# Dummy matmuls before and between the first transposes of a two-layer mixer trunk: 13 become 16 + 2 + 4

## The chip, the cores and the metric

One core of a Trainium2 chip. The metric is the device time of one launch in microseconds, the median of several launches.

## The reference

A decoder trunk of two layers on 256 tokens of width 1024, batch 1. Each layer normalizes the stream, projects it once, feeds four token mixers from the projection (sparse attention, a gated short convolution, stick-breaking attention and an S5 state-space layer), gates and merges them, projects the sum and adds it back:

```python
h = rms_norm(x, g)
proj = h @ w_in          # split by columns among the mixers, the silu gates and the merge gates
y = [nsa(...), conv(...), stickbreak(...), s5(...)]     # each [1, 256, 256]
m = sum(sigmoid(gate_i) * ((y_i * silu(z_i)) @ w_branch_i) for i in range(4))
x = x + m @ w_out
```

The S5 mixer multiplies its input into a complex state (`bu`), runs a diagonal recurrence over the 256 positions, multiplies the states back and sums them (`s5acc`), and passes the result through a GLU.

## The kernel before

All matrix products are taken in a split form: each float32 operand is cut into a high part (`hi`, a cast) and a low part (`lo`, operand minus `hi`), and three products hi·hi, hi·lo, lo·hi are summed. The weights stream in slots of 512 KB (536 KB for the first two) through the DMA queue of SyncE (SP): `raw`, three buffers; the cast to `hi` (L148, ScalarE or VectorE) and the subtraction `lo` (L150, VectorE, some on GpSimd), five buffers each. Slots 0 and 1 hold the query weights `q`, 2 and 3 `ksw`, and so on. Slot 0 holds the rows of the weights that meet the first 512 columns of h, slot 1 the other 512.

The beginning of layer 0: x is loaded, `norm_square` and `norm_scale` make the normalized h for the first 128 rows (t = 0) in two halves of 512 columns (L553, VectorE); `norm_transpose` turns each half by four transposing matmuls (`hT`, L561), copies the result out as `hh` (L564, ScalarE) and subtracts to get `hl` (L565, VectorE). Then the products of q and ksw (L488) begin, and the second 128 rows (t = 1) follow. While TensorE has nothing to do at the start, 13 matmuls of a zero tile (`warm_ps`, 128x128 by 128x512, bf16) run on it. Their output is not used.

In the middle of a layer the S5 mixer forms a chain over eight blocks, in the order 00, 01, 04, 05, 02, 03, 06, 07: TensorE makes `bu` (L855), VectorE multiplies it by tables (`s5a`, `s5b`, L858 and L859), GpSimd adds (L286, L289), VectorE scans (L865) and multiplies (`cy`, L868 and L871), GpSimd adds again, and after four blocks TensorE sums them into `s5acc` (L883). GpSimd starts the adding of a block's `s5a` behind the `cy` of the block before. After both groups of four come `s5yT`, `s5y`, the GLU (`glu`, L905) and `s5th` (L914). `spawn(prepare(l + 1))` behind it loads the next layer's parameters (`pk`) and computes its tables on GpSimd, ScalarE and VectorE, in among layer 0's merging (`mg`: merge gates; `br`: branch projections; `g`: the gates' tanh, L928; `mt`, L946).

The orders of the DMA queue (SP) and of GpSimd are those in which the program was written. The orders of TensorE, VectorE and ScalarE are chosen by a scheduler that plays the program through on a cost model of its own and always takes the ready instruction it judges best; every instruction added to one of these engines can move others.

Of the kernel before, what the change touches and what calls it, by code (L numbers as in the profile page):

```python
# [9 lines left out]
F32 = mybir.dt.float32  # L10
# [7 lines left out]
P = 128  # L18
# [17 lines left out]

_PK = [("a_re", 8), ("a_im", 8), ("ldt", 8), ("pe", 32), ("b_re", 128), ("b_im", 128), ("c_re", 128), ("c_im", 128),
       ("d", 2), ("glub", 4), ("convw", 6), ("w2", 64), ("qkg", 256), ("qkgs", 256)]
WARM = 13
PK, _o = {}, 0  # L40
for _n, _w in _PK:
    PK[_n] = (_o, _w)
# [135 lines left out]
def tile_hybrid_trunk(ctx: ExitStack, tc: tile.TileContext, x, pos, cst, msk, wq, ws, ng, pk, w1, gw, out):  # L178
    nc = tc.nc
    V, A, G, T = nc.vector, nc.scalar, nc.gpsimd, nc.tensor  # L180
# [11 lines left out]
    pj = ctx.enter_context(tc.tile_pool(name="pj", bufs=4, space=PSUM))  # L192
# [24 lines left out]
    def small(name, cols):  # L217
        t = sp.tile([P, 16], F32, tag="s", name=name)
        return t[:, :cols]
# [39 lines left out]
    ident = C("ident")  # L259
# [295 lines left out]
    def norm_transpose(l, t, act):  # L555
        hh, hl = act
        h = Ls[l]["norm"][t][0]
        for c in range(2):
            ps = wk.tile([P, 4, P], F32, tag="w", name=f"hT{l}{t}{c}")
            for k in range(4):  # L560
                T.transpose(ps[:, k, :], h[:, (4 * c + k) * P:(4 * c + k + 1) * P], ident)  # L561
            dst = (slice(None), slice(4 * c, 4 * c + 4), slice(t * P, (t + 1) * P))
            with tc.high_priority():
                A.copy(hh[dst], ps)  # L564
                V.tensor_sub(hl[dst], ps, hh[dst].bitcast(F32))  # L565
# [449 lines left out]

    warm = cp.tile([P, P], BF16, name="warm")
    V.memset(warm, 0.0)
    ps = pj.tile([P, 512], F32, tag="pj", name="warm_ps")
    for _ in range(WARM):
        T.matmul(ps, lhsT=warm, rhs=warm[:, None, :].to_broadcast([P, 4, P]), start=True, stop=True)  # L1020
    sin0 = small("sin0", 1)
    A.activation(sin0, halfpi, AF.Sin)
    act = new_act(0)
# [3 lines left out]
    for c in range(2):  # L1027
        norm_square(0, 0, c, 2)
    norm_scale(0, 0)
    norm_transpose(0, 0, act)  # L1030
    W.advance(-3)
    rope = rope_tables()
# [16 lines left out]
    for l in range(DEPTH):  # L1049
# [36 lines left out]
        qs = get_n(l, "q")  # L1086
        n_part(l, "q", qs, act, 0, q_done, WQ, by_pass=True)
        norm_transpose(l, 1, act)
        ks = get_n(l, "ksw")
        pump()  # L1090
# [61 lines left out]
        if more:  # L1152
            W.advance((l + 1) * NSLOT - 1)
        out_part(l, 3, s3, mx, 1, lambda: norm_transpose(l + 1, 0, act) if more else None)
        done_n(l, ("wo", 3))
        if more:
# [85 lines left out]
def build(arrays):  # L1242
    import concourse.bacc as bacc

    nc = bacc.Bacc("TRN2", target_bir_lowering=False, num_devices=1)
    args = [nc.dram_tensor(f"in_{k}_dram", a.shape, mybir.dt.from_np(a.dtype), kind="ExternalInput").ap()
            for k, a in arrays.items()]
    args.append(nc.dram_tensor("out_0_dram", (S, D), F32, kind="ExternalOutput").ap())
    with tile.TileContext(nc, schedule_with_timeline_sim=True) as tc:
        tile_hybrid_trunk(tc, *args)  # L1250
    return nc
# [9 lines left out]
```

## Time and profile before

| | us |
|---|---|
| median of 3 runs | 568.13 (567.42 to 570.21) |
| the profiled execution | 566.94 |
| its span | 565.2 |
| TensorE busy in it | 546.1 |
| TensorE's mean granted clock in it | 0.987 of full speed |

The span is the time between the first and the last instruction of the profiled execution; 1.74 us lie around it. Times in the rows below are microseconds from the start of the span. A granted clock of 1.00 is TensorE's level of 2.4 GHz, 0.50 that of 1.2 GHz. A bracket such as `[2.56 <-DVE h L553]` says that the engine sat idle for 2.56 us before the row and that VectorE's h ended it.

### The profile page before, as it was taken

What the parts mean: (1) busy time and instruction counts of PE and PEld (TensorE: products, weight loads), DVE (VectorE), ACT (ScalarE), POOL (GpSimd) and SP (SyncE); (2) the same over time, 40 slices, a digit from 0 to 9 for tenths busy, and PEclk for the clock granted to TensorE, in tenths of its full rate; (3) what the DMA queues carried; (4) which work ended last, traced back from release to release, by engine and by line L of the source; (5) the groups of instructions that cost most, each with busy time, mean ns of one, the idle gap of its engine ahead of it and who ended that gap; (6) DMA issues with size and microseconds to landing.
All of it is one profiled execution on the core that took longest, in us unless ns stands there. A gap on an engine that the chain in (4) does not pass through costs nothing.

```text
span 565.2 us, 11178 instructions
## 1 busy us (share of the span) xinstructions
PE 546.1 (97%) x4417; PEld 510.1 (90%) x4417; DVE 440.1 (78%) x654; ACT 264.0 (47%) x436; POOL 275.3 (49%) x309
## 2 busy tenths in 40 slices
PE   6999999999899899799999999999999999999997
PEld 3898988889799799799998998889889999999997
DVE  3999776888989764888769985968898777687772
ACT  4656353654334444654454555454434345444440
POOL 7949536634665529597033776713335620243200
PEclk7899999999899999999999999999999999999999
DMA  7584154544444636465556725364344635555541
GB/s 257 194 279 157 42 201 119 199 153 146 150 126 137 223 134 206 149 199 180 190 171 213 220 72 164 112 222 135 112 154 147 202 139 180 187 188 186 188 135 53
DMA packets 28853, 93.54 MB, mean 166 GB/s; under 512 B 3968, under 2 KB 5248, under 8 KB 28800
## 3 DMA queue, kind: packets, MB, share of 16 engines
q1 hardware_dynamic: 28800, 92.82, 50.5%
q8 instruction: 35, 0.57, 0.4%
q14 instruction: 18, 0.15, 0.1%
HBM read 88.61 MB, written 1.05 MB: 159 GB/s over the span
## 4 chain that ended last, share of the span: by engine, by line
PE 71%; DVE 11%; POOL 9%; issue 4%; DMA 2%; ACT 2%; SPq 1%; DVEq 0%; POOLq 0%; ACTq 0%
PE mg L498 24%; PE wo L488 7%; PE br L943 7%; PE z L498 4%; DVE lo L150 2%; PE s5u L498 2%; PE sbv L488 2%; PE bg L498 2%; PE sc L709 2%; PE xin L498 2%; PE sbk L498 2%; PE nsacc L746 2%; DVE s5b L865 1%; POOL cy L286 1%; PE cg L498 1%
## 5 line engine op out<-in xcount | busy, mean ns | idle before, releaser
L150 DVE TENSOR_TENSOR lo<-raw,hi 128x1024 fp32r<-128x1024 f32 (+1 forms) x152 | 209.1, 1379 | 43.8 <-ACT hi L148 43.4
L148 ACT CAST hi<-raw 128x1024 fp32r<-128x1024 f32 (+1 forms) x154 | 161.2, 1050 | 173.8 <-PE mg L498 52.8
L498 PE MATMUL mg<-hh,hi 128*128 128x256 f32 x512 | 145.1, 283 | 0.4 <-DVE mt L946 0.4
L498 PE MATMUL mg<-hh,lo 128*128 128x256 f32 x512 | 144.6, 283 | 0.0
L498 PE MATMUL mg<-hl,hi 128*128 128x256 f32 x512 | 144.5, 282 | 0.0
L498 PEld LDWEIGHTS mg<-hh,hi 128*128 128x128 f32 x512 | 97.0, 190 | 3.0 <-issue 2.4
L498 PEld LDWEIGHTS mg<-hl,hi 128*128 128x128 f32 x512 | 97.4, 190 | 1.2 <-issue 1.2
L498 PEld LDWEIGHTS mg<-hh,lo 128*128 128x128 f32 x512 | 97.0, 189 | 1.2 <-issue 1.2
L286 POOL TENSOR_TENSOR mt<-mt,mt 128x512 f32<-128x512 f32 x12 | 19.0, 1585 | 70.6 <-DVE mt L946 70.6
L289 POOL TENSOR_TENSOR cy<-cy 128x256 f32<-128x256 f32 x16 | 18.2, 1138 | 57.9 <-DVE cy L871 54.2
L488 PE MATMUL wo<-hi,mx 128*128 128x256 f32 x256 | 45.6, 281 | 0.0
L488 PEld LDWEIGHTS wo<-hi,mx 128*128 128x128 f32 x256 | 39.2, 188 | 0.0
L943 PE MATMUL br<-oh,hi 128*128 128x256 f32 x128 | 36.0, 282 | 2.4 <-ACT g L928 2.4
L498 PE MATMUL z<-hh,hi 128*128 128x256 f32 x128 | 36.1, 282 | 0.0
L498 PE MATMUL z<-hl,hi 128*128 128x256 f32 x128 | 36.1, 282 | 0.0
L498 PE MATMUL z<-hh,lo 128*128 128x256 f32 x128 | 36.0, 281 | 0.0
L943 PE MATMUL br<-ol,hi 128*128 128x256 f32 x128 | 36.0, 281 | 0.0
L943 PE MATMUL br<-oh,lo 128*128 128x256 f32 x128 | 36.0, 281 | 0.0
L488 PE MATMUL wo<-lo,mx 128*128 128x256 f32 x128 | 35.3, 282 | 0.0
L865 DVE TENSOR_TENSOR_SCAN s5b<-r,s5a 128x256 f32<-128x256 f32 x32 | 20.3, 677 | 11.8 <-POOL s5a L289 11.8
L286 POOL TENSOR_TENSOR s5a<-s5a,s5b 128x256 f32<-128x256 f32 x16 | 20.2, 1262 | 17.1 <-DVE s5b L859 17.1
L943 PEld LDWEIGHTS br<-oh,hi 128*128 128x128 f32 x128 | 24.1, 189 | 2.6 <-ACT g L928 2.6
(333 smaller groups left out, 1417.4 us busy)
## 6 DMA issues: line engine op xcount, KB each, us to landing
raw<-in_ws_dram SPq DMA_DIRECT2D x152, 512.0 KB, 3.7
raw<-in_wq_dram SPq DMA_DIRECT2D x4, 536.0 KB, 5.0
w<-in_w_dram SPq DMA_DIRECT2D x4, 512.0 KB, 5.7
b<-bh SPq DMA_DIRECT2D x16, 64.0 KB, 2.0
u<-uh SPq DMA_DIRECT2D x16, 64.0 KB, 2.0
gw<-in_gw_dram SPq DMA_DIRECT2D x2, 512.0 KB, 5.4
out_dram<-xs SPq DMA_DIRECT2D x8, 128.0 KB, 1.7
xs<-in_x_dram SPq DMA_DIRECT2D x2, 256.0 KB, 3.2
```

Source lines behind the costliest of these rows:

```text
L148: self.nc.scalar.copy(hi[:, :w], t[:, :w])
L150: sub.tensor_sub(lo[:, :w], t[:, :w], hi[:, :w].bitcast(F32))
L286: G.tensor_add(o, a, b)
L289: G.tensor_sub(o, a, b)
L488: T.matmul(ps[:, :width], lhsT=act(4 * h + kk)[ia][:, tt], rhs=w[iw][:, kk, :], start=n == 0, stop=n == last)
L498: T.matmul(ps, lhsT=w[:, k, :], rhs=a[:, k, :], start=n == 0, stop=n == last)
L709: T.matmul(sc[kh].rearrange("p (b g k) -> p b g k", b=nb, g=2)[:, :, g, :], lhsT=qT[iq][rows[kh], g, t * P:(t + 1) * P], rhs=kT[ik][rows[k ...
L746: T.matmul(acc[rows[kh], :, t * P:(t + 1) * P], lhsT=v[:, c, b * P + 64 * kh:b * P + 64 * kh + 64], rhs=ps4[kh][:, c, 2 * i:2 * i + 2, :], ...
L865: V.tensor_tensor_scan(y[:, ri, :], L["r"][:, pr:pr + 1].to_broadcast([P, S]), a[:, ri, :], 0.0, op0=ALU.mult, op1=ALU.add)
L943: T.matmul(ps[:, j, :], lhsT=w[:, 2 * m + k, :], rhs=a[:, k, :], start=n == 0, stop=n == 5)
```

## The change

`WARM` becomes three numbers. Sixteen dummy matmuls stand at the start in place of 13; two more are issued behind the fourth transpose of h's first half, four more behind the fourth of its second half, for layer 0 and t = 0 alone. `tc.issue_after(last.ins)` tells the scheduler not to issue them ahead of that transpose.

```diff
-WARM = 13
+WARM = 16, 2, 4
@@ norm_transpose
             for k in range(4):
-                T.transpose(ps[:, k, :], h[:, (4 * c + k) * P:(4 * c + k + 1) * P], ident)
+                last = T.transpose(ps[:, k, :], h[:, (4 * c + k) * P:(4 * c + k + 1) * P], ident)
+            if l == t == 0:
+                with tc.issue_after(last.ins):
+                    keep_busy(WARM[1 + c])
@@
-    ps = pj.tile([P, 512], F32, tag="pj", name="warm_ps")
-    for _ in range(WARM):
-        T.matmul(ps, lhsT=warm, rhs=warm[:, None, :].to_broadcast([P, 4, P]), start=True, stop=True)
+    warm_ps = pj.tile([P, 512], F32, tag="pj", name="warm_ps")
+
+    def keep_busy(n):
+        for _ in range(n):
+            T.matmul(warm_ps, lhsT=warm, rhs=warm[:, None, :].to_broadcast([P, 4, P]), start=True, stop=True)
+
+    keep_busy(WARM[0])
```

The order of SP and of GpSimd stays as it was, row for row. The other three engines change theirs in layer 0; layer 1 is the same.

**TensorE, the first transposes.** In the rows below the figure behind `hT` is layer, t and half, `hi0` and `lo0` are the parts of weight slot 0, and `x4` stands for four matmuls. Before:

```order
L1020 MATMUL warm_ps_138<-warm_136 128x512
L561 MATMUL hT000_181<-cs_94,h00_173 128x128 x4
L561 MATMUL hT001_188<-cs_94,h00_173 128x128 x4
L488 MATMUL q00_285<-hi0_195,hh0_154 128x268 x4
L488 MATMUL q00_285<-lo0_196,hh0_154 128x268 x4
```

and of the change, in the same place:

```order
L561 MATMUL hT000_184<-cs_94,h00_176 128x128 x4
L1025 LDWEIGHTS warm_136
L1025 MATMUL warm_ps_138<-warm_136 128x512
L1025 LDWEIGHTS warm_136
L1025 MATMUL warm_ps_138<-warm_136 128x512
L561 MATMUL hT001_193<-cs_94,h00_176 128x128 x4
```

Two dummies now stand between the halves, and four more behind the second one, ahead of the first product of q.

**TensorE, ahead of the first product that needs lo3.** Before, the last rows ahead of it and itself:

```order
L488 MATMUL ksw00_343<-hi3_273,hh0_154 128x256
L488 MATMUL q01_384<-hi0_195,hh0_154 128x268
L488 MATMUL q01_384<-lo0_196,hh0_154 128x268
L488 MATMUL ksw01_428<-hi2_241,hh0_154 128x256
L488 MATMUL ksw01_428<-lo2_242,hh0_154 128x256
L488 MATMUL ksw00_343<-lo3_274,hh0_154 128x256
```

and of the change:

```order
L488 MATMUL q01_393<-hi1_225,hl0_158 128x268
L488 MATMUL ksw01_437<-hi2_250,hh0_157 128x256
L488 MATMUL ksw01_437<-lo2_251,hh0_157 128x256
L488 MATMUL ksw01_437<-hi2_250,hl0_158 128x256
L488 MATMUL ksw01_437<-hi2_250,hh0_157 128x256
L488 MATMUL ksw00_352<-lo3_283,hh0_157 128x256
```

Ahead of this product and behind the first that needs lo2 stand 16 matmuls before and 45 with the change: products of the second 128 rows (q01, ksw01) that stood behind it have moved ahead of it.

**VectorE, the first block of the S5 chain.** Before, the weight subtraction ahead of it is that of slot 30:

```order
L150 TENSOR_TENSOR lo29_1719<-raw29_1607,hi29_1718 128x1024
L790 SCALAR_TENSOR_TENSOR cvy0_1461<-cvu0_1460,pk0_119,cvy0_1461 128x255 x2
L790 SCALAR_TENSOR_TENSOR cvy0_1461<-cvu0_1460,pk0_119,cvy0_1461 128x254 x2
L795 TENSOR_TENSOR cvy0_1461<-bg0_1463,cvy0_1461 128x512
L150 TENSOR_TENSOR lo30_1761<-raw30_1643,hi30_1760 128x1024
L858 TENSOR_TENSOR s5a00_1596<-bu00_1593,Ct0_600 128x512
```

and of the change that of slot 28:

```order
L150 TENSOR_TENSOR lo27_1649<-raw27_1528,hi27_1648 128x1024
L793 SCALAR_TENSOR_TENSOR cvy0_1470<-cvu0_1469,pk0_119,cvy0_1470 128x255 x2
L793 SCALAR_TENSOR_TENSOR cvy0_1470<-cvu0_1469,pk0_119,cvy0_1470 128x254 x2
L798 TENSOR_TENSOR cvy0_1470<-bg0_1472,cvy0_1470 128x512
L150 TENSOR_TENSOR lo28_1691<-raw28_1573,hi28_1690 128x1024
L861 TENSOR_TENSOR s5a00_1605<-bu00_1602,Ct0_609 128x512
```

The chain's first instruction moves ahead of two weight slots. In the stream of TensorE `bu00` stands 41 matmuls earlier, while the products of the weights around it stand later by 8 to 20.

**TensorE, the fourth block's part of s5acc.** Before, `cy05` is first wanted here:

```order
L498 MATMUL mg021_2030<-hh0_154,lo35_1948 128x256
L498 MATMUL mg021_2030<-hh0_154,hi35_1947 128x256
L883 MATMUL s5acc0_1977<-cy05_1871,CM_105 32x256
L883 MATMUL s5acc0_1977<-cy04_1793,CM_105 32x256
L498 MATMUL mg021_2030<-hl0_155,hi35_1947 128x256
```

and of the change here:

```order
L498 MATMUL mg020_1955<-hl0_158,hi33_1883 128x256
L498 MATMUL mg020_1955<-hh0_157,lo33_1884 128x256
L886 MATMUL s5acc0_1986<-cy05_1880,CM_105 32x256
L886 MATMUL s5acc0_1986<-cy04_1802,CM_105 32x256
L498 MATMUL mg020_1955<-hh0_157,hi33_1883 128x256
```

It moves up by 63 matmuls. The last block of the second group (`cy07`) moves up by 22 and the GLU by 24; from the branch products `br` on, the stream is the one before.

## Rows read from the trace of the kernel before

**Rows 1.** The chain of work that ended last, followed back from the last instruction: its shares of the span by engine.

```profile
PE 71%; DVE 11%; POOL 9%; issue 4%; DMA 2%; ACT 2%; SPq 1%; DVEq 0%; POOLq 0%; ACTq 0%
```

**Rows 2.** The waits of TensorE (PE): tile and line, what it waited for; total us, times, longest.

```profile
PE hT L561 <- DVE h L553: 4.1, 3, 2.6
PE s5acc L883 <- POOL cy L289: 3.8, 2, 1.9
PE br L943 <- ACT g L928: 2.4, 1, 2.4
PE ksw L488 <- DVE lo L150: 1.2, 1, 1.2
...
PE sc L709 <- DVE qTl L601: 0.4, 1, 0.4
PE s5acc L883 <- POOL cy L286: 0.4, 1, 0.4
```

**Rows 3.** Timeline of PE, the first 24 us: start, length, engine, line, operation, count; in brackets the idle time ahead of it and what ended it.

```profile
0.98 4.58 PE L1020 MATMUL warm_ps<-warm 128*128 128x512 bf16 x13 [0.98 <-DVE warm L1017]
8.13 1.11 PE L561 MATMUL hT<-cs,h 128*128 128x128 f32 x4 [2.56 <-DVE h L553]
9.62 1.12 PE L561 MATMUL hT<-cs,h 128*128 128x128 f32 x4 [0.38 <-DVE h L553]
11.70 1.26 PE L488 MATMUL q<-hi,hh 128*128 128x268 f32 x4 [0.97 <-ACT hh L564]
...
18.99 0.39 PE L488 MATMUL ksw<-lo,hh 128*128 128x256 f32 x1
...
22.30 0.39 PE L488 MATMUL ksw<-lo,hh 128*128 128x256 f32 x1 [1.15 <-DVE lo L150]
```

**Rows 4.** Stretches of the span: its bounds and length; busy time of PE, PEld, DVE, ACT and POOL, each with its instructions; then PE's granted clock, the DMA share and GB/s.

```profile
7.80:17.90 10.10, 8.43 (x35) 7.46 (x36) 7.21 (x12) 6.43 (x11) 7.96 (x14) 0.50 0.82 288
18.10:24.00 5.90, 4.60 (x37) 4.16 (x36) 5.90 (x10) 2.89 (x7) 5.49 (x7) 1.00 0.64 214
24.00:46.00 22.00, 22.00 (x189) 22.00 (x187) 21.74 (x59) 13.41 (x23) 14.54 (x15) 1.00 0.69 236
60.00:140.00 80.00, 80.00 (x623) 70.58 (x618) 61.07 (x94) 36.57 (x69) 38.85 (x49) 1.00 0.48 152
...
151.10:154.40 3.30, 3.30 (x17) 3.30 (x17) 3.30 (x5) 1.45 (x3) 1.92 (x2) 0.50 0.58 185
```

**Rows 5.** Timeline of ScalarE (ACT) in the first stretch, the same columns.

```profile
10.08 1.08 ACT L148 CAST hi<-raw 128x1072 fp32r<-128x1072 f32 x1 [4.36 <-DMA raw<-in_wq_dram]
11.07 1.07 ACT L564 CAST hh<-hT 128x512 fp32r<-128x512 f32 x2
```

**Rows 6.** Timeline of VectorE (DVE) up to 52 us, the same columns.

```profile
17.73 1.20 DVE L150 TENSOR_TENSOR lo<-raw,hi 128x1024 fp32r<-128x1024 f32 x1
18.85 1.58 DVE L345 TENSOR_TENSOR gS<-qk,ropeS 128x192 f32<-128x192 f32 x2
20.36 0.76 DVE L346 TENSOR_TENSOR gS<-qk,ropeS 128x64 f32<-128x64 f32 x1
21.04 1.21 DVE L150 TENSOR_TENSOR lo<-raw,hi 128x1024 fp32r<-128x1024 f32 x1
...
23.83 2.40 DVE L574 TENSOR_SCALAR ssq<-ssq 128x4 f32<-128x4 f32 x1
...
49.99 0.42 DVE L601 TENSOR_TENSOR qTl<-qTp,qT 128x256 fp32r<-128x256 f32 x1
```

**Rows 7.** Timeline of PE, the waits at the S5 accumulations and the first row of block 05's part (159.53).

```profile
150.02 0.62 PE L883 MATMUL s5acc<-cy,CM 128*32 128x256 f32 x2 [1.93 <-POOL cy L289]
...
159.53 0.63 PE L883 MATMUL s5acc<-cy,CM 128*32 128x256 f32 x4
...
192.33 0.63 PE L883 MATMUL s5acc<-cy,CM 128*32 128x256 f32 x4 [1.84 <-POOL cy L289]
```

**Rows 8.** Timeline of GpSimd (POOL), the start of a block's cy: blocks 00, 01, 05, 02 and 07.

```profile
133.26 0.74 POOL L289 TENSOR_TENSOR cy<-cy 128x256 f32<-128x256 f32 x1 [4.61 <-DVE cy L871]
...
140.82 0.74 POOL L289 TENSOR_TENSOR cy<-cy 128x256 f32<-128x256 f32 x1 [2.72 <-DVE cy L871]
...
156.74 1.59 POOL L289 TENSOR_TENSOR cy<-cy 128x256 f32<-128x256 f32 x1 [3.72 <-PE mg L498]
...
164.12 1.66 POOL L289 TENSOR_TENSOR cy<-cy 128x256 f32<-128x256 f32 x1 [2.72 <-DVE cy L871]
...
190.71 1.57 POOL L289 TENSOR_TENSOR cy<-cy 128x256 f32<-128x256 f32 x1 [4.38 <-DVE cy L871]
```

**Rows 9.** Timeline of DVE, its part of the S5 chain.

```profile
115.72 1.22 DVE L150 TENSOR_TENSOR lo<-raw,hi 128x1024 fp32r<-128x1024 f32 x1
...
125.77 0.68 DVE L858 TENSOR_TENSOR s5a<-bu,Ct 128x512 f32<-128x512 f32 x1
...
138.14 1.27 DVE L865 TENSOR_TENSOR_SCAN s5b<-r,s5a 128x256 f32<-128x256 f32 x2 [1.33 <-POOL s5a L289]
...
203.90 0.87 DVE L914 SCALAR_TENSOR_TENSOR s5th<-glu,pk,s5th 128x256 f32<-128x256 f32 x2
```

**Rows 10.** The chain that ended last, pieces in order of time: start, us, what.

```profile
204.80 2.94 DMA pk<-in_pk_dram
...
224.12 0.42 ACT cos L402
```

## The prediction

> **What bounds the kernel now.** I read the chain that ended last first, by engine: TensorE has 71% of it, VectorE, GpSimd and the rest share what is left [rows 1]. A change to the order therefore pays where TensorE waits, and I took its waits next [rows 2]: 4.1 us for the first transposes, 1.0 for the first product of q (its bracket is in [rows 3]), 1.2 for a weight's low part, 0.4 at the first scores, 3.8 and 0.4 at the S5 sums and 2.4 at the branch products. All else is products, one behind the other: from 60 to 140 us TensorE is busy for 80.00 of 80 us [rows 4]. So nearly all that an earlier start gives must come through the few waits, and each of them must be asked for itself.
>
> The first 24 us come next [rows 3]. The dummies end at 5.56 us, the first transposes begin at 8.13 behind h, the second at 9.62, q at 11.70. The granted clock is 0.50 from 7.8 to 17.9 us and 1.00 behind it [rows 4]: the transposes and the first products run at 1.2 GHz. The reader is to see what q waits for: the cast of the first weights begins when their transfer has landed, at 10.08 us, and the casts of the transposed h follow it at 11.07 [rows 5]. The idle time at the beginning belongs to loads and casts, not to TensorE. Faster transposes bring q forward by nothing.
>
> **The change, part by part.** Three more dummies at the start: at 4.58 us for 13, thus 0.35 each, they end about 1.1 us later, at 6.6, ahead of the transposes at 8.13. Cost nothing; h covers them, and with that cover gone it would be 1.1.
>
> Two and four between the transposes and q: idle there is 0.38 and 0.97, together 1.35 us [rows 3]. The price of a dummy at either clock I bound by rows. At 1.2 GHz 35 matmuls take 8.43 us, 0.24 each, at 2.4 GHz 37 take 4.60, 0.12 each [rows 4]; a dummy has about twice their columns, so 0.24 or 0.48. Six take 1.4 us at the high clock, which the idle time holds, and 2.9 at the low one: then q begins up to 1.5 us late. I take the high clock: the low one came behind the idle time of 2.56 us ahead of the first transpose [rows 3], which shrinks to about 1.5.
>
> What the clock gives: the products from 11.70 to 17.9 then need half their time, but they are fed by casts and subtractions that keep their times, and lo2 (17.73), the table products gS (18.85 and 20.36) and lo3 (21.04) follow one another on VectorE without a gap [rows 6]. TensorE is at the first product of lo2 at 18.99 before [rows 3], and would be at about 18.75 after. What counts is what stands behind it. Before, 16 products follow and TensorE then waits 1.15 us for lo3; after, 45 do, 45 x 0.12 = 5.4 us, to 24.1 us, and lo3 comes at about 23.5 (two more subtractions of h, 1.2 us, stand ahead of it). The wait is filled, and at 24.1 us TensorE has 73 products done where it had 56: 17 x 0.12 = 2.0 us ahead.
>
> The Trainium skill (TensorE: Matmul & The Clock Gate, Terms) prices time at the low clock as that time by the share of pulses withheld, half of it here; the sum by it would be rival (d).
>
> How much of the 2.0 us is left at the first scores: VectorE is busy for 21.74 of the 22 us from 24 on [rows 4], so its own work decides. The scores need qTl of the second 128 rows, which is done at 50.41 [rows 6]; TensorE had been there 0.4 us earlier [rows 2], at 50.0. In the new order one weight subtraction (1.21) less stands ahead of it: 49.2. The upper bound is that also the 2.40 us at 23.83 shrink to the 0.2 that so small an operation can take: 47.0. The scores stand 17 products (2.0 us) earlier in TensorE's stream, where it was at 48.0 before; with the 0.4 that it then lost, the lead is 48.4 less the start: between -0.8 and 1.4 us. I take the middle, 0.3.
>
> The S5 chain: s5a00 goes from behind lo30 to behind lo28, which began at 115.72 [rows 9]. Weight products stand up to 20 (2.4 us) later in the new stream and free buffers later: lo28 at 115.72 + 2.4 - 0.3 = 117.8, done at 119.0. So s5a00 starts at 119.0 and not at 125.77, 6.8 us earlier. From it to the first cy on GpSimd are 7.5 us, and 7.5 from that to the next (133.26, 140.82) [rows 8]; four steps give 149.0 for block 05 where it was 156.74. Its first half ends 1.6 later, at 150.6.
>
> TensorE wants it 63 matmuls (7.4 us) earlier than at 159.53 [rows 7]. With the lead (0.3), without the wait of 1.93 and without the low-clock stretch from 151.1 to 154.4 (half of 3.3, 1.65 us [rows 4]) it is there at 148.3. It waits 2.3 us, against 1.93 before. That stretch followed a wait of 1.93, and I let it follow this one too.
>
> The second group: with block 05 done on VectorE at 149.0, the new order puts two weight subtractions (1.22 each), two operations of the size of s5a (0.68) and s5a02, s5b02 ahead: 5.2 us, then 4.9 us from GpSimd's start to the next scan (133.26 to 138.14 [rows 8, 9]) of which GpSimd's half, 2.5, is needed, a scan of 1.27, a subtraction of 1.22 and the cy pair of 1.3. Block 02's cy starts at 160.5, where it was 164.12: of 7.7 us 3.6 are left. Laid on in the same way, three further blocks bring 07's cy to 189.3, 1.4 us ahead of its 190.71. So the second sum ends 1.4 us earlier. It stands 22 matmuls (2.6 us) earlier in the stream, so 2.6 us more work is left behind it: 1.2 us lost. Bounds: 5.3 us earlier (no wait left) and 1 later (a lead of -0.8 and one more subtraction ahead).
>
> The branch products wait 2.4 us for a gate behind a long chain: s5th at 203.90, then the load of the next layer's parameters at 204.80, GpSimd's tables, and ScalarE's cos at 224.12 [rows 9, 10]. That chain starts 1.4 us earlier, and TensorE comes 1.2 later: 2.6 against 2.4, the wait is gone. Bounds: 0 to 2.4.
>
> Sum: -1.4 + 2.6 - 2.4 = -1.2 us. On the profiled execution's 566.94 that is 565.7; the median of the runs is 1.2 above that execution, so 566.9.
>
> **The rivals.** (a) The chain keeps its lead of over 5.3 us through the second group, since VectorE's subtractions fit between the scans as they did before (steps of 7.5 us [rows 8]). Then the waits of 1.84 and 0.37 go as well: lead 0.3, less 0.4 for block 05, and 2.2 and 2.4 for the waits: 4.5, 563.6. Against it stands the order, which puts more ahead of the scans than before.
>
> (b) The change doesn't do what it says: the clock is low at 8 us and the six dummies run at 1.2 GHz, and q is 1.2 us late. The lead is then gone, the chain's 1.4 us shrink to 0.2, and the sum is 0.0: 568.1. For it speaks that the clock fell with 13 dummies, and that transposes at 8.13 and 9.62 ran while it stayed low. [...]
>
> (c) Slower: the pieces of attention (scores, their transposes and sums) stand 2.0 to 4.8 us earlier in the stream between 50 and 120 us. TensorE takes its stream in order; where their makers on ScalarE and VectorE are not earlier by as much, it waits where it waited for nothing (80.00 of 80 us). Beyond 4.1 us of such waits the kernel is slower by over 0.5%; at 5 it takes 571.8. Against it: ScalarE is busy for 37 and VectorE for 61 of these 80 us [rows 4].
>
> (d) All of the low stretch reaches the end: half of 10.1 us at 0.50 [rows 4] is 5.1, so 563.0. VectorE's 21.74 of 22 us speaks against it.
>
> **How the numbers follow.** The forecast has 0.45, (a) 0.25, (b) 0.15, (c) 0.12, (d) 0.03. The forecast's own range is 564.7 to 569.3: the chain's end 3.6 us earlier (as at block 02) or 1 later. The range of 8 in 10 reaches from 562.6, (a) with a lead at its upper bound, to 569.9, where waits of (c) take 3 us from the forecast. About 0.5%, 2.8 us, is what a measurement can tell from no change: below 565.3 is faster, above 571.0 slower. Faster: (a), (d) and a fifth of the forecast, 0.37. Slower: (c) and a little of (b), 0.14. The rest, 0.49, is the same.
>
> **What would show it.** In the new profile: a granted clock of 1.00 from 8 to 18 us (or 0.50, then (b)); no wait for lo3 near 22 us; the first scores before 50.1; s5a00 near 119; a wait of 2 to 3 us at 148 for block 05, one of about 3.5 near 188 for block 07; none at the branch products. The prediction is wrong if no wait is left at block 07, or if new ones stand between 50 and 140 us.

## The result and the profile after

The changed kernel takes 564.68 us (median of five, 564.43 to 565.75) where the one before took 568.13: a ratio of 0.9942 (95% interval 0.9922 to 0.9962), 3.45 us faster. The forecast was 566.9, with 562.6 to 569.9 around it. Beside these medians the two profiled executions are only 1.2 us apart: 566.94 before and 565.75 after, the slowest of its five.

TensorE's waits after, to be held against [rows 2]:

```profile
PE s5acc L886 <- POOL cy L289: 4.8, 2, 3.1
PE hT L561 <- DVE h L553: 3.0, 3, 1.7
PE vsw L488 <- DVE sqq L591: 1.0, 1, 1.0
...
PE ksw L488 <- DVE lo L150: 0.6, 1, 0.6
PE q L488 <- ACT hh L567: 0.5, 1, 0.5
...
PE s5acc L886 <- POOL cy L286: 0.4, 1, 0.4
```

Gone are the branch products' wait of 2.4 us, that for lo3 (the 0.6 left under `ksw` is for lo2) and that of the first scores. The S5 sums wait longer, 4.8 us for 3.8. New are two waits ahead of products of `vsw`, which follow those of `ksw`: 1.04 us at 28.65 and 0.46 at 32.2; both stand in every profile of this order. The first stage, which answers to [rows 3]:

```profile
0.98 6.28 PE L1025 MATMUL warm_ps<-warm 128*128 128x512 bf16 x16 [0.98 <-DVE warm L1020]
8.91 0.66 PE L561 MATMUL hT<-cs,h 128*128 128x128 f32 x4 [1.65 <-DVE h L553]
9.40 0.59 PE L1025 MATMUL warm_ps<-warm 128*128 128x512 bf16 x2
9.84 0.60 PE L561 MATMUL hT<-cs,h 128*128 128x128 f32 x4
10.27 1.03 PE L1025 MATMUL warm_ps<-warm 128*128 128x512 bf16 x4
11.82 0.77 PE L488 MATMUL q<-hi,hh 128*128 128x268 f32 x4 [0.53 <-ACT hh L567]
...
19.20 0.39 PE L488 MATMUL ksw<-lo,hh 128*128 128x256 f32 x1 [0.55 <-DVE lo L150]
```

The clock in it and near 150 us, and two of the stretches in between, which answer to [rows 4]:

```profile
7.80:17.90 10.10, 7.57 (x46) 5.51 (x47) 7.87 (x11) 7.11 (x13) 8.55 (x14) 1.00 0.66 251
24.00:46.00 22.00, 20.50 (x173) 20.13 (x171) 21.94 (x60) 13.51 (x23) 16.61 (x17) 1.00 0.72 248
60.00:140.00 80.00, 80.00 (x611) 70.66 (x610) 62.10 (x95) 38.80 (x71) 41.42 (x52) 1.00 0.47 149
147.00:157.00 10.00, 6.92 (x32) 4.88 (x32) 8.62 (x13) 1.63 (x3) 3.99 (x4) 0.66 0.42 140
```

The clock is 1.00 from 7.8 to 17.9 us where it was 0.50, so the dummies do hold it. And yet q begins at 11.82 instead of 11.70: what feeds it has not moved. From 24 to 46 us TensorE is busy for 20.50 us, where it was busy for all 22 [rows 4]: the two new waits. Near 150 us the clock has fallen again, for 6.8 us in this execution (a mean of 0.66 over these ten). The S5 chain on GpSimd (blocks 00, 05, 02, 07), against [rows 8], and TensorE's waits for blocks 05 and 07, against [rows 7]:

```profile
126.89 1.66 POOL L289 TENSOR_TENSOR cy<-cy 128x256 f32<-128x256 f32 x1 [4.25 <-DVE cy L874]
...
149.27 1.58 POOL L289 TENSOR_TENSOR cy<-cy 128x256 f32<-128x256 f32 x1 [2.78 <-DVE cy L874]
...
160.22 0.74 POOL L289 TENSOR_TENSOR cy<-cy 128x256 f32<-128x256 f32 x1 [4.43 <-DVE cy L874]
...
188.72 2.17 POOL L289 TENSOR_TENSOR cy<-cy 128x256 f32<-128x256 f32 x1 [3.77 <-DVE cy L874]
```

```profile
150.90 1.07 PE L886 MATMUL s5acc<-cy,CM 128*32 128x256 f32 x4 [3.08 <-POOL cy L289]
...
190.95 0.62 PE L886 MATMUL s5acc<-cy,CM 128*32 128x256 f32 x4 [1.71 <-POOL cy L289]
```

### The profile page after: what moved, and what is told of

Same layout as the page of the kernel before. It is cut to its first block, busy times and chain, and to the rows that moved or that the text cites. A ratio compares the mean times of both kernels' runs of the same rounds, so it can differ in the third digit from the quotient of the medians.

```text
span 564.0 us, 11204 instructions
## 1 busy us (share of the span) xinstructions
PE 547.5 (97%) x4426; PEld 508.5 (90%) x4426; DVE 436.7 (77%) x654; ACT 265.0 (47%) x436; POOL 276.4 (49%) x309
## 3 DMA queue, kind: packets, MB, share of 16 engines
HBM read 88.61 MB, written 1.05 MB: 159 GB/s over the span
## 4 chain that ended last, share of the span: by engine, by line
PE 76%; POOL 7%; DVE 7%; DMA 3%; issue 3%; ACT 1%; SPq 1%; DVEq 0%; POOLq 0%; ACTq 0%
PE mg L498 25%; PE wo L488 7%; PE br L946 7%; PE z L498 6%; PE sbv L488 2%; PE s5u L498 2%; PE cg L498 2%; PE xin L498 2%; PE bg L498 2%; PE sbk L498 2%; PE sc L712 2%; DMA raw<-in_ws_dram 2%; DVE lo L150 2%; PE s5acc L886 2%; PE nsacc L749 2%
## 5 line engine op out<-in xcount | busy, mean ns | idle before, releaser
L289 POOL TENSOR_TENSOR cy<-cy 128x256 f32<-128x256 f32 x16 | 21.2, 1325 | 60.5 <-DVE cy L874 60.5
L498 PEld LDWEIGHTS z<-hl,hi 128*128 128x128 f32 x128 | 24.2, 189 | 0.8 <-issue 0.8
```

Source lines behind the costliest of these rows:

```text
L289: G.tensor_sub(o, a, b)
L498: T.matmul(ps, lhsT=w[:, k, :], rhs=a[:, k, :], start=n == 0, stop=n == last)
```

## The experiments

Two theories stood against the one in the prediction (order and clock together): the order alone, and the clock alone. They can be told apart, since the scheduler has just two answers to the numbers used here: the order of the change, row for row on all three engines (11 dummies at the start and none behind; 2 and none; 16, 2, 4), or that of before (12 and none; 13 and none; 16, 1, 4).

**The order alone.**

```diff
-WARM = 16, 2, 4
+WARM = 11, 0, 0
```

> 11 dummies at the start, none behind. The scheduler then gives the three engines the order of the change, row for row, without its dummies, so this is the order alone. Theory (order and clock are both needed: the order moves the S5 chain ahead, the clock gives the lead of 0.3 to 0.6 us that it starts from): low clock from 8 to 18 us, first scores at 48.5 to 50, cy07 on GpSimd at 189.5 to 190.5, 567 to 568 us. Rival 1 (order alone): as the change, 564.7. Rival 2 (clock alone): as before, 568.1.

Measured: 563.65 us, ratio 0.9914 (0.9884 to 0.9945) to the kernel before on that chip (568.77). The first stage of it, and its first score:

```profile
8.01 0.66 PE L561 MATMUL hT<-cs,h 128*128 128x128 f32 x4 [2.24 <-DVE h L553]
9.61 1.11 PE L561 MATMUL hT<-cs,h 128*128 128x128 f32 x4 [0.95 <-DVE h L553]
11.82 1.26 PE L488 MATMUL q<-hi,hh 128*128 128x268 f32 x4 [1.10 <-ACT hh L567]
...
47.84 0.38 PE L712 MATMUL sc<-kT,qT 64*128 64x256 f32 x1
```

The transposes of the second half and the products of q take as long as before (four products of q in 1.26 us in both; 0.77 in the change), so the clock is low there; still the first scores begin at 47.84, as in the change. The order alone brings the whole gain, and the theory's "both" falls.

**The dummies alone.**

```diff
-WARM = 16, 2, 4
+WARM = 16, 1, 4
```

> 16 dummies, then 1 and 4. One fewer between the halves, and the scheduler keeps the order of before, row for row: the dummies alone. Theory: granted clock 1.00 from 8 to 18 us, but TensorE then waits longer for lo3 (about 22.3 us, the wait grows from 1.2 to some 2.5 us), the first scores stay at 50.5, and the time is that of before, 567.5 to 568.5. Rival 1 (order alone): 568.1 too. Rival 2 (clock alone): 564.7.

Measured: 568.8, ratio 0.9998 (0.9976 to 1.0021). The first stage's clock, and the first score:

```profile
7.80:17.90 10.10, 7.64 (x46) 5.52 (x46) 8.03 (x12) 6.91 (x13) 8.31 (x13) 1.00 0.81 297
```

```profile
49.84 0.38 PE L712 MATMUL sc<-kT,qT 64*128 64x256 f32 x1 [0.38 <-DVE qTl L604]
```

A clock of 1.00 through the first stage, and the scores wait for qTl at 49.84 with the same bracket as before. The dummies themselves are worth nothing. The time is what the first theory and rival 1 expected, 0.3 us above the theory's range; two details of the theory missed: the wait for lo3 is 1.16 us and not 2.5, and the scores begin at 49.84 and not at 50.5.

**One dummy more, and nearly none.** The kernel of the first experiment with 12 dummies for 11, and one with 2:

```diff
-WARM = 16, 2, 4
+WARM = 12, 0, 0
```

> 12 dummies at the start, none behind: one more than in e1_order_11. With it the scheduler falls back to the order of before, row for row. Order alone as the cause: 567.5 to 569, that is 4 to 6 us above e1, for one dummy at a place where TensorE is idle anyway. If it were the dummies or the clock: equal to e1 within 0.5 us.

```diff
-WARM = 16, 2, 4
+WARM = 2, 0, 0
```

> 2 dummies in all; the scheduler gives the order of the change. TensorE then goes into the first transposes and q at 1.2 GHz for longer than in any other kernel. If VectorE's queue sets the first scores (order alone), they begin within 0.7 us of the 47.8 of e1 and the time is 563.5 to 565. If the clock of the first 18 us has a share in the gain: first scores at 49 or later, and 565.5 to 568.

Measured: 567.7 with 12 (ratio 0.9977, 0.9954 to 1.0000) and 564.44 with 2 (0.9918, 0.9897 to 0.9939). One dummy more than 11, at a place where TensorE is idle anyway, costs 4 us (563.65 and 567.7, on two chips on which the kernel before took 568.77 and 568.78), by the order that it brings. And without any warm-up to speak of:

```profile
0.99 1.03 PE L1025 MATMUL warm_ps<-warm 128*128 128x512 bf16 x2 [0.99 <-DVE warm L1020]
8.94 1.97 PE L561 MATMUL hT<-cs,h 128*128 128x128 f32 x8 [6.92 <-DVE h L553]
11.64 1.26 PE L488 MATMUL q<-hi,hh 128*128 128x268 f32 x4 [0.73 <-ACT hh L567]
...
47.60 0.38 PE L712 MATMUL sc<-kT,qT 64*128 64x256 f32 x1
```

TensorE is idle for 6.9 us, the transposes and q start at the low clock (four products of q in 1.26 us again), q at 11.64, and the scores are at 47.60, no later than in the change (47.75). No time of the first 24 us at the low clock reaches the scores.

**Where the clock falls later.** The profiled executions differ by more than the forecast, so both kernels were profiled again, unchanged. For the change:

> The changed kernel once more, for a second profile of it and of where its clock falls. Theory: 564.4 to 565.4; a fall of the clock near 150 us behind the wait for block 05, 3.4 to 6.8 us long, and a wait of 1.5 to 3.5 us at block 07 that is the longer, the shorter that stretch is, since the S5 chain and not TensorE sets when the second sum ends. Rival: the low stretch costs time of its own, and the time goes up by half of it.

> The changed kernel beside it on the same chip, and a third profile of it: 563 to 565; second sum done at 190.6 to 192.6.

and for the kernel before:

> The kernel before, a second profile: does its clock fall behind the wait for block 07 (as in both other kernels with its order, near 193 us), or near 151 us as in the first profile? If a fall near 193 is its usual one, the span is 566 to 568 and the second sum ends at 193.3 to 194.5, and the first profile was a fast one for it.

> The kernel before, a third profile, for the same question: where its clock falls, and when the second sum ends.

Measured: the change 563.06 (ratio 0.9907, 0.9873 to 0.9941), 1.3 us below the range that I gave, and 563.84 (0.9930, 0.9903 to 0.9957), inside it. The last profile of before, its second sum and the stretch behind it:

```profile
193.10 1.07 PE L883 MATMUL s5acc<-cy,CM 128*32 128x256 f32 x4 [3.46 <-POOL cy L289]
...
195.25 1.06 PE L883 MATMUL s5acc<-cy,CM 128*32 128x256 f32 x2
```

```profile
192.00:200.00 8.00, 6.90 (x29) 5.06 (x30) 2.49 (x5) 1.56 (x2) 4.04 (x3) 0.57 0.41 133
```

and the same of the change's last profile:

```profile
189.14 0.63 PE L886 MATMUL s5acc<-cy,CM 128*32 128x256 f32 x4 [0.84 <-POOL cy L289]
```

```profile
192.00:200.00 8.00, 8.00 (x70) 8.00 (x70) 5.04 (x7) 3.94 (x6) 2.10 (x1) 1.00 0.57 179
```

Before waits 3.46 us for block 07, the clock then falls, and from 192 to 200 us it gets 29 products done where the change gets 70. With the two orders' other kernels there are five profiles of each order (us; the second sum's end is the start of its last row, the tail runs from there to the start of TensorE's last row):

| order of | profile | wait for 05 | wait for 07 | second sum's end | clock low near 193 | tail | wait at br | span |
|---|---|---|---|---|---|---|---|---|
| before | before | none | 1.84 | 194.00 | no | 367.85 | 2.40 | 565.2 |
| before | 16, 1, 4 | 0.33 | 2.33 | 193.35 | 3.4 us | 371.03 | 2.69 | 567.7 |
| before | 12 | 0.29 | 2.35 | 193.46 | 3.4 us | 369.11 | 2.47 | 565.9 |
| before | before, 2nd | none | 2.99 | 194.34 | 3.4 us | 368.55 | 2.5 | 566.2 |
| before | before, 3rd | 0.31 | 3.46 | 195.25 | 6.8 us | 369.78 | 2.57 | 568.3 |
| change | change | 3.08 | 1.71 | 192.62 | no | 368.04 | none | 564.0 |
| change | 11 | 3.08 | 1.97 | 191.53 | no | 367.53 | none | 562.4 |
| change | change, 2nd | 3.06 | 0.82 | 190.64 | no | 367.06 | none | 561.0 |
| change | 2 | 3.09 | 2.02 | 191.77 | 3.4 us | 369.20 | none | 564.3 |
| change | change, 3rd | 3.09 | 0.84 | 190.81 | no | 366.70 | none | 560.8 |

The means: the second sum ends at 194.1 in the one order and 191.5 in the other, 2.6 us earlier; the tail takes 369.3 and 367.7, 1.6 less; the span is 566.7 and 562.5, 4.2 less. My expectation for the two extra looks at before held: a fall near 193 is the usual case, four of five, and the profile that the prediction rests on is the one without it (the third profile's span and second sum lie above the ranges that I gave).

The clock falls behind the wait at the branch products too, in two of the five profiles of the order of before: in the third of before (233.7 to 237.1 us), and in that with 16, 1 and 4 dummies, whose two stretches are:

```profile
193.60:196.90 3.30, 3.30 (x14) 2.72 (x13) 0.99 (x3) 1.20 (x2) 2.02 (x1) 0.50 0.54 180
231.20:234.40 3.20, 2.71 (x12) 2.71 (x13) 3.20 (x9) 1.37 (x2) 0.00 (x0) 0.50 0.54 169
```

That accounts for the tail. Between the second sum's end and TensorE's last row the clock is low for 4.1 us on average in the order of before and for 0.7 in that of the change, all of it at these two places. With half of the low time taken off, the tails are 367.2 and 367.4 us.

The wait for block 07 goes with a row of GpSimd: the first of block 07's cy, here of the last profile of the change and of the last of before.

```profile
188.03 1.05 POOL L289 TENSOR_TENSOR cy<-cy 128x256 f32<-128x256 f32 x1 [3.77 <-DVE cy L874]
```

```profile
190.33 2.71 POOL L289 TENSOR_TENSOR cy<-cy 128x256 f32<-128x256 f32 x1 [4.37 <-DVE cy L871]
```

In all ten profiles VectorE begins the subtraction of a weight's low part within 0.4 us of the start of this row, and the row takes between 1.04 and 2.71 us. Within each order the wait is the longer, the longer the row: 0.82 and 0.84 us for rows of 1.04 and 1.05 and 1.71 to 2.02 for rows of 2.17 and 2.18 in the change's; 1.84 to 2.35 for rows of 1.57 and 2.99 and 3.46 for rows of 2.71 in that of before.

So it is not shown what the low stretch near 150 us costs. The change's three profiles have the same program, and the one with 6.8 us of it ends its second sum 1.8 to 2.0 us later than those with 3.4, but its row of GpSimd is also 1.1 us longer; with 11 and with 2 dummies, where the stretch is 3.4 us and the row 2.18, the sum ends 0.9 to 1.1 us before it. That much may be the stretch. That the wait for 07 be longer where the stretch is shorter, as I expected, is refuted.

**Shorter, later, filled: three ways to gain more.** The low parts of slots 43 and 46 on GpSimd:

```diff
-    W = Weights(nc, tc, raw, hip, lop, wq, ws, 3, 5, (4, 79, 81, 95), (17, 87))
+    W = Weights(nc, tc, raw, hip, lop, wq, ws, 3, 5, (4, 43, 46, 79, 81, 95), (17, 87))
```

> The changed kernel with the low parts of weight slots 43 and 46 made on GpSimd, so that they no longer stand on VectorE ahead of cy06 and cy07 (1.2 us each). Theory (the S5 chain sets the end of the second sum): cy07 starts up to 2.4 us earlier, the wait at block 07 of 1.7 and 0.4 us goes, 562.6 to 563.6. Rival (TensorE's own products set it, the wait only moves): 564.4 to 565.4. Second rival: the 2.4 us that GpSimd takes for a low part come between its own adds, and cy07 is not earlier.

Measured: 566.02 (0.9958, 0.9936 to 0.9980), 3 us slower than the change of the same chip. GpSimd's rows, and the scans of blocks 06 and 07 on VectorE:

```profile
182.77 3.35 POOL L150 TENSOR_TENSOR lo<-raw,hi 128x1024 fp32r<-128x1024 f32 x1
189.11 0.72 POOL L289 TENSOR_TENSOR cy<-cy 128x256 f32<-128x256 f32 x1 [3.00 <-DVE cy L874]
```

```profile
173.83 1.27 DVE L868 TENSOR_TENSOR_SCAN s5b<-r,s5a 128x256 f32<-128x256 f32 x2 [1.43 <-POOL s5a L289]
...
183.81 3.43 DVE L868 TENSOR_TENSOR_SCAN s5b<-r,s5a 128x256 f32<-128x256 f32 x2
```

The subtraction fits between GpSimd's own adds, but while it runs the scan of 07 takes 3.43 us instead of 1.27, and 07 starts at 189.11, later than in the change. So the theory was not tested by it: the chain did not get shorter. The second rival is right in its result, by another way. The lost 3 us, though, do not lie at the second sum: it ends at 191.11 in this profile, within the change's 190.64 to 192.62, and the row of GpSimd there takes 0.72 us, as no subtraction of VectorE begins near it. The two waits of TensorE that no profile of the change has:

```profile
PE br L946 <- ACT g L931: 1.8, 1, 1.8
PE mg L498 <- POOL lo L150: 1.1, 1, 1.1
```

The branch products wait for the gate again, at 231.40, and the merge gates wait for one of the moved low parts, at 186.17. Behind the wait at the branch products the clock is low from 232.0 to 235.4 us. The tail is 371.70 us, longer than any of the table. This profile is of the slowest of the kernel's twelve executions (568.24).

The sum one and two steps later in the program:

```diff
-            yield 2
+            yield 3 if l == pair == 0 else 2
```

> The changed kernel with the S5 sum of the first group written one step later in layer 0. Block 05's part stands 13 products (1.5 us) later in TensorE's stream, block 07's 27 (3.2 us), bu02 27. Theory (where the sum stands decides how much of the chain's lateness TensorE waits for): the wait for block 05 falls from 3.1 to about 1.5 us, cy07 is 1 to 2 us later since one more subtraction stands ahead of s5a02, the wait for block 07 stays under 1 us, 1 to 2 us faster than the change; no wait at the branch products as long as s5th stays before 203. Rival (all products are in the way anyhow): as the change, within 0.5 us.

> The same with the sum two steps later: block 05's part 38 products (4.5 us) later than in the change, block 07's 52 (6.1 us). Theory: no wait for block 05, so no low clock behind it if that wait is what brings it; none for block 07; but cy07 and s5th are 3 us or more later, and the branch products wait again for the gate, 1 to 4 us. About the time of the change, 562.5 to 566. Rival: the fall of the clock near 150 us comes without the wait too.

Measured: 564.81 (0.9933, 0.9909 to 0.9958) and, with 4 for 3, 567.67 (0.9984, 0.9967 to 1.0001). The waits of the first, and the clock of the second:

```profile
PE s5acc L886 <- POOL cy L289: 4.6, 3, 2.4
...
PE br L946 <- ACT g L931: 2.2, 1, 2.2
```

```profile
140.00:157.00 17.00, 17.00 (x146) 15.86 (x145) 14.44 (x18) 6.73 (x9) 7.00 (x6) 1.00 0.50 152
```

In the first the wait for block 05 shrinks to 1.77 as expected, but that for 07 grows to 2.41 and the branch products wait 2.2 us again: what was won in one wait comes back in the two behind it, and the expected 1 to 2 us are not there. In the second TensorE is busy for 17.00 of 17 us around 150 and the clock stays at 1.00, while in every profile with a wait of 3.1 us there it fell. Its chain is late, though: 07 starts at 192.45, TensorE waits 7.9 us in all for the sums (4.7 in layer 0, 3.2 in layer 1), and the time is 1.7 us above what I had allowed. Block 07's part still waits, for 1.33 us, and the branch products don't; I had expected the opposite of both. And a wait of this length does not always bring a fall: block 06's part of the same kernel waits longer, and the clock stays.

```profile
186.66 0.62 PE L886 MATMUL s5acc<-cy,CM 128*32 128x256 f32 x2 [3.33 <-POOL cy L289]
```

```profile
186.00:196.00 10.00, 7.63 (x56) 6.29 (x56) 7.06 (x8) 4.30 (x5) 7.22 (x7) 1.00 0.70 234
```

The wait for block 05 filled with dummies:

```diff
+                        if (l, pair, half, ri, j) == (0, 0, 1, 0, 1):
+                            with tc.issue_after(last.ins):
+                                for _ in range(24):
+                                    T.matmul(yacc[32 * q:32 * q + 32, half, :], lhsT=warm[:, :32],
+                                             rhs=warm[:, None, :].to_broadcast([P, 2, P]), start=True, stop=True,
+                                             tile_position=(0, 32 * q))
```

> The changed kernel with 24 more dummies (32 rows by 256 columns, bf16, into the place that block 05's sum then overwrites) ahead of block 05's part of the S5 sum. The rest of the order is the change's but for 14 rows. If the idle wait there (3.1 us in the change) is what lets the clock fall near 150 us: no fall there, the second sum ends 1 to 2 us earlier than in the change of the same chip, 1 to 2 us faster. If VectorE's and GpSimd's chain alone sets the second sum: the clock stays high and the time doesn't move by more than 0.7 us, as the wait for block 07 takes back what TensorE wins. If so narrow a dummy doesn't count as activity: the clock falls as before.

Measured: 565.9 (0.9948, 0.9921 to 0.9974), 2 us slower than the change beside it (563.84). The clock:

```profile
140.00:151.00 11.00, 8.61 (x78) 7.33 (x77) 8.90 (x12) 2.60 (x4) 6.68 (x6) 1.00 0.33 110
151.60:154.60 3.00, 3.00 (x12) 2.27 (x11) 2.76 (x4) 0.39 (x1) 0.00 (x0) 0.50 0.65 227
```

It falls all the same in this execution, behind a wait that is still 2.39 us. Whether these dummies don't hold the clock or the rest of the wait was enough stays open. But in two of the kernel's twelve executions the granted clock is 1.00 over the whole span, and they take 562.78 and 562.82 us, no less than the fastest of the change beside it (562.43): without a fall, too, the fill gains nothing. Nor did it change the wait alone. Among the rows that moved are VectorE's scans of block 02, whose cy starts at 161.84, 2.3 us later than in the change beside it:

```profile
161.84 0.74 POOL L289 TENSOR_TENSOR cy<-cy 128x256 f32<-128x256 f32 x1 [5.81 <-DVE cy L874]
```

Neither this nor any other kernel beats the change by more than its runs scatter.

## Why the prediction was right, and where it was not

**The first stage.** Right: the clock of 1.00, the dummies hidden, lo3 no longer waited for, the first scores earlier than 50.1 (47.75, a lead of 0.7 for the 0.3 I took). Wrong in its reason: I let the lead come from TensorE's 2.0 us and priced rival (b) as its loss at a low clock. The kernels with 11 and 2 dummies have the low clock and the lead. What I should have carried to its end was my own sentence that VectorE's work decides; then the clock has no price here, and (b) no mechanism. TensorE does run ahead by the new order, with 83 matmuls done at 24 us for 71 (dummies left out), but it gives that back in the two waits ahead of `vsw` that I had not foreseen, 1.5 us together. By the Trainium skill's price (TensorE: Matmul & The Clock Gate, Terms) the low stretch comes to an estimated 5.1 us. The dummies alone, which take it away, gave 0.0 us: here the products in it waited for casts and subtractions, and the price did not apply.

**The S5 chain.** Right, nearly to the row: block 05's cy at 149.27 (149.0), 02's at 160.22 (160.5), 07's at 188.72 (189.3), a wait for 05 of 3.08 (2.3), none at the branch products. In that one pair of executions the sum of -1.2 us is what was measured: the second sum ends 1.38 us earlier (1.4), TensorE's last row 1.19. That it fits so closely is luck: 07's cy is 2.0 us earlier and not 1.4, but its first row on GpSimd took 2.17 us for 1.57 and gave 0.6 back. The wait for 07 was to be about 3.5 us and was 1.71 (0.82 to 2.02 in the five profiles): in this pair TensorE comes to it some 2 us later than I took it to, as the wait for 05 was 0.8 us longer and the low stretch 6.8 us and not 3.4. Over five profiles of each order 07's cy is 2.2 us earlier (188.1 against 190.3) and the sum's end 2.6: the term was undersized by 0.8 and 1.2.

**The step that failed** is the one behind the sum: "the median of the runs is 1.2 above that execution, so 566.9". It took the difference between that execution and the median for an offset that both kernels share. It is no such offset: the profile of before was 1.2 us faster than its kernel's median, that of the change 1.1 slower than its own. In the order of before TensorE mostly waits 2.3 us or more for block 07, and the clock then falls; in that of the change it waits less, and the clock falls in one of five. In two of five it also falls behind the wait at the branch products, which the change takes away. The tail, which I had at 0.2 us longer (+2.6 - 2.4), is 1.6 shorter; without the half clock it would be 0.2 longer, so the term that I put at nothing is the clock in the tail, 1.7 us. In the profile that I read the wait for 07 was 1.84 and no fall followed; it had one near 151 us instead, so I knew that a wait of this size can have one behind it, and put its price only at the place where I saw it. Term by term: -2.6 and -1.6, against -1.4 and +0.2, 4.2 us and not 1.2.

Over the whole execution the clock makes less of the difference, since the change has its own fall near 150 us every time. Counted from 24 us on, the low time falls from 6.1 to 4.8 us on average (worth half, 0.7 us), TensorE's waits fall from 10.5 to 8.1 (2.3 us), and at 24 us the change has 10.8 matmuls more behind it on average (1.3 us at 0.12 each): together 4.3 us.

**The chances.** No change, the likeliest by my numbers with 0.49, did not come; the range held. Rival (a) had the right size (563.6) by the wrong way: of the chain's lead of over 5.3 us 2.2 are left at 07's cy, and waits for 07 remain. Rival (c), attention's pieces waiting between 60 and 140 us, is refuted: TensorE is busy for 80 of 80 us there in the change too, and the first wait behind the scores is block 05's.

## What to carry to other kernels

Where a scheduler chooses the order, an edit can act through the order alone: make the edit with another number that leaves the order as it was, and the order without the edit, before giving the gain to a cause. Take several profiles of the kernel before when its runs scatter by more than the effect sought, since a fall of the clock that most executions have can be missing in a single lucky one. A stage that looks slow on one engine is worth nothing while another engine's queue sets the next hand-over.

## What the hardware showed that was not expected

TensorE's clock fell behind a wait of 3.1 us near 150 us in each of the six profiles that have one, behind one of 1.9 near the same place in two of five with the other order, and neither behind one of 1.77 there nor in the one profile without a wait. The length of the wait alone does not tell: waits of 1.60 us for block 07 and of 1.84 at the branch products had a fall behind them, waits of 1.97 for block 07, of 2.40 to 2.55 at the branch products and of 3.33 for block 06 had none. In one and the same program the stretch at half clock lasted 3.4 us in some executions and 6.8 in others.

A VectorE scan of 1.27 us took 3.43 while GpSimd made a low part (3.35 us, 182.77 to 186.12), and the same pair appears at the start: a VectorE operation on four elements per partition takes 2.40 us [rows 6], beside a low part of 2.42 on GpSimd that began 0.04 us before it, and the same operation later in that kernel takes 0.16. It goes the other way too: GpSimd's row of 0.72 us took 1.04 to 2.71 where VectorE's low part began within 0.4 us of it.
